# A hybrid decoder layer on one core: side work placed by a running plan of all engines in place of fixed delays, block states by scans, the samples' convolution taps by products, and no arithmetic left on GpSimd in the output projection

## The chip, the cores and the metric

The kernel runs on one core of one Trainium2 chip. The metric is device microseconds of one execution. The kernel before takes 1282.72 us, the median of 3 runs (1280.19 to 1284.27). A core has five instruction queues that run side by side and meet only at semaphores: PE (TensorE: matmuls and transposes), DVE (VectorE), ACT (ScalarE), POOL (GpSimd) and SP (SyncE, here DMAs alone). Each queue runs its own instructions in the order in which they were written. Arithmetic between engines goes through SBUF; PE writes PSUM banks, which ACT and DVE empty. DMAs are issued from SP and from POOL.

## The reference

One layer (`DEPTH = 1`) over 1024 prompt positions and 8 samples of 4 positions, width 1024. Both share all weights.

```python
mod = silu(c) @ w_ada + b_ada                       # shift, scale, gate, twice
h = rmsnorm(x, g_pre_mix) * (1 + sc1) + sh1
z = h @ w_in                                        # 24 blocks of 128 columns
za, zq, zf, zi, zg, zc = split(z)
ya = u * (tril(w_s) @ layernorm(v) + b_s)           # chunked gMLP, u, v = gelu(za)
# HGRN2, 8 heads of 64x64: per chunk with decay products b
#   o = (q*exp(b)) @ S + tril((q*exp(b)) @ (k*exp(-b)).T) @ v
#   S = exp(b_last) * S + (k*exp(b_last - b)).T @ v
yb = rmsnorm(o) * silu(zg)
yc = silu(layernorm(conv31(a * sigmoid(gate)) + b_dw))    # 31 taps per channel
y = concat(ya, yb, yc) @ w_out
x = x + gt1 * rmsnorm(y, g_post_mix)
h = rmsnorm(x, g_pre_mlp) * (1 + sc2) + sh2
x = x + gt2 * rmsnorm(square(relu(h @ w_up)) @ w_down, g_post_mlp)
```

The new states of HGRN2, the last convolution rows and the gMLP's v rows of the samples are returned too.

## The kernel before

All activations lie with features on the partitions: a tile of 128 x 1056 holds 128 features of the 1024 prompt and 32 sample positions, cut into three chunks `c` of 352 columns. Every large product is computed as three matmuls on a high and a low half of each operand (hi*hi, hi*lo, lo*hi), so a block of 128 output features and one chunk is 8 x 3 = 24 matmuls `pmt` of 352 columns. I count the program's place by these matmuls: 1728 of them make the input projection (24 blocks x 3 chunks), 576 the output projection (8 x 3, chunk by chunk, so chunk 0 ends at 1920, chunk 1 at 2112, chunk 2 at 2304), and 4608 the MLP. The first up-products of chunk 0 run from 2304 to 2400, those of chunk 1 from there.

Around this stream lies the side work, all of it written as Python generators in named queues (`queues`, `add_task`): the adaLN products (`ada`), for each of four pairs of HGRN2 heads the decay products (`stage`), transposes (`turned`: `vtps`, `ktps`), scores, states and outputs (`recur`: `sc`, `us`, `ob`, `uss`, `os_`) and the norm (`head_norm`: `gnps`), the convolution (`conv_taps`, `conv_tail`), the gMLP (`gmlp`), and after the output projection `after_mix` for each chunk: sum of squares `tot`, a matmul with ones (`stps`), square root on ACT, reciprocal and products on DVE, addition of x by an accumulating DMA from POOL (L1412), a copy to DRAM (L1415), squares `sq` of the sum, their fold, a second `stps`, then `h2{c}hi` and `h2{c}lo`, which the up-products read.

`product8` writes the 24 matmuls in four pieces of six and calls `step` after each. `step(t)` (L164) moves a clock forward by the time of a piece and resumes those generators whose due time has come and whose engines have credit. A generator says with `yield 11.0`, `yield settle(3.0, "act", "pool")` or `yield 6.5` after how many microseconds it wants to go on; `settle` adds what an engine is behind by its credit. `Metered` (L38) charges each instruction a price from its size (`dve_price`, `ActPrice`, `pool_price`, `pe_price`). So the place of a transpose or a small matmul in PE's queue comes from a fixed delay, not from when its operands are ready. If it stands too early, PE waits there, and with it the large products behind it.

PSUM banks for side work come from a pool of five (`pb`, tag `b`), those for `pmt` from a pool of three (`pm`). Small tiles (`rs`, tag `rs`) rotate over three buffers.

Two pieces of arithmetic that the change touches: the state of each 64-position block is computed on DVE in 16 steps of one instruction per pair (`S[:, b] = D64[b] * S[:, b-1] + u[b]`, read straight from PSUM, L1180 on), and copied by ACT in four parts for each head. And for the samples each of the 31 taps of the convolution is one DVE instruction on 8 x 4 columns beside the prompt's one of 1024 columns (L805 on). In the output projection the squares of a block's result are added up on POOL (`add_square(tot, ps, m, POOL)`), and a third of each of the chunks 0 and 1 is scaled there (`scaled(..., (2,))`).

## Time and profile before

| what | value |
|---|---|
| median of 3 runs | 1282.72 us |
| profiled execution, its own time | 1286.04 us |
| its span, first to last instruction | 1284.2 us |
| mean granted TensorE clock | 0.985 |
| PE busy | 1243.9 us (97%) |
| DVE busy | 729.9 us (57%) |
| ACT busy | 480.8 us (37%) |
| POOL busy | 91.0 us (7%) |

The profile is of one execution; the span leaves out 1.8 us of its own time. Nearly all instructions carry one line (L56), that of the helper `Metered`, so groups are told apart by the names of their tiles. A row of a group gives engine, operation, output<-inputs, shapes, count, busy time in all, mean nanoseconds of one, and the idle time ahead of them with what ended it. The busy time of PE counts a matmul until its modelled end, so neighbours overlap: what tells of PE is where it is idle, and how far apart matmuls start. PEclk is the clock that was granted to it, as a share of full speed.

### The profile page before, as it was taken

The page shows a single profiled execution, that of the slowest core. Times are in us where ns is not written, and L with a number is a line of the kernel's source. Part 1 is how long each engine was busy: PE and PEld are TensorE (multiplying, and loading weights), DVE is VectorE, ACT ScalarE, POOL GpSimd, SP SyncE. Part 2 cuts the span into 40 slices and gives each one's busy share as a digit, 9 for nine tenths or more (in the row PEclk, how much of TensorE's full clock was granted, in tenths as well). Part 3 has the DMA queues.
Part 4 walks back from the last instruction along what each step waited for, and adds up shares of the span by engine and source line. Part 5 has one row for each costly group of instructions (what it writes and reads, how often), then busy time and mean ns, then how long its engine had stood idle before and what let it go on. Part 6 is the DMA issues. An engine that isn't in the chain of part 4 may idle for free.

```text
span 1284.2 us, 20789 instructions
## 1 busy us (share of the span) xinstructions
PE 1243.9 (97%) x8770; PEld 1199.8 (93%) x8770; DVE 729.9 (57%) x1182; ACT 480.8 (37%) x890; POOL 91.0 (7%) x123
## 2 busy tenths in 40 slices
PE   9999999998999998799999999999999999999995
PEld 7888988997999998799999999999999999999994
DVE  5799898879768657745343333333333333433366
ACT  6512544665754745445320220320311311311333
POOL 0000020212010233000000000000000000000001
PEclk9999999999899999799999999999999999999998
DMA  9557240111111467143211111111111111110218
GB/s 363 177 146 291 74 184 24 36 58 46 34 43 52 150 176 207 48 128 107 82 50 50 36 48 50 50 50 36 47 50 50 36 48 50 50 50 34 90 18 207
DMA packets 39246, 113.24 MB, mean 88 GB/s; under 512 B 9952, under 2 KB 12160, under 8 KB 39024
## 3 DMA queue, kind: packets, MB, share of 16 engines
q1 hardware_dynamic: 34832, 99.22, 23.0%
q0 software_dynamic: 4320, 12.68, 4.4%
q8 instruction: 69, 1.13, 0.4%
q14 instruction: 25, 0.20, 0.0%
HBM read 101.75 MB, written 10.14 MB: 87 GB/s over the span
## 4 chain that ended last, share of the span: by engine, by line
PE 81%; DVE 8%; ACT 6%; issue 2%; DMA 2%; POOL 1%; SPq 0%; DVEq 0%; ACTq 0%; POOLq 0%
PE pmt L56 74%; PE adaps L56 1%; PE stps L56 1%; DVE acc L56 1%; DMA raw<-in_wup 1%; DMA o<-in_xT 1%; PE sc L56 1%; DVE wlo L56 1%; DVE o L56 1%; PE pmt L673 1%; DVE sq L56 1%; ACT sq L56 1%; ACT whi L56 1%; DVE R L56 1%; DVE q L56 1%
## 5 line engine op out<-in xcount | busy, mean ns | idle before, releaser
L56 PE MATMUL pmt<-ah,whi 128*128 128x352 f32 (+2 forms) x744 | 241.4, 324 | 0.0
L56 PE MATMUL pmt<-al,whi 128*128 128x352 f32 (+2 forms) x744 | 240.1, 323 | 0.3
L56 PE MATMUL pmt<-ah,wlo 128*128 128x352 f32 (+2 forms) x744 | 240.1, 323 | 0.0
L56 ACT CAST whi<-raw 128x1024 fp32r<-128x1024 f32 (+2 forms) x113 | 114.3, 1014 | 261.0 <-PE pmt L56 261.0
L56 DVE TENSOR_TENSOR acc<-acc,pmt 128x352 f32<-128x352 f32 (+2 forms) x176 | 87.8, 503 | 167.7 <-PE pmt L56 167.7
L56 DVE TENSOR_TENSOR wlo<-raw,whi 128x1024 fp32r<-128x1024 f32 (+2 forms) x113 | 136.5, 1210 | 70.0 <-ACT whi L56 69.9
L56 DVE TENSOR_TENSOR rsq<-relu 128x352 f32<-128x352 f32 x84 | 44.2, 526 | 188.4 <-ACT relu L56 188.4
L56 PEld LDWEIGHTS pmt<-al,whi 128*128 128x128 f32 x744 | 140.0, 188 | 1.6 <-DVE al L56 0.8
L56 PEld LDWEIGHTS pmt<-ah,whi 128*128 128x128 f32 x744 | 139.7, 188 | 1.1 <-ACT ah L56 0.3
L56 PEld LDWEIGHTS pmt<-ah,wlo 128*128 128x128 f32 x744 | 139.9, 188 | 0.4
L56 ACT ACTIVATE relu<-pmt 128x352 f32<-128x352 f32 x96 | 44.6, 464 | 237.1 <-PE pmt L56 237.1
L56 PE MATMUL pmt<-h22hi,wlo 128*128 128x352 f32 x256 | 82.6, 323 | 0.0
L56 PE MATMUL pmt<-h22hi,whi 128*128 128x352 f32 x256 | 82.5, 322 | 0.0
L56 PE MATMUL pmt<-h22lo,whi 128*128 128x352 f32 x256 | 82.3, 322 | 0.0
L56 PE MATMUL pmt<-h21lo,whi 128*128 128x352 f32 x232 | 75.3, 324 | 2.5 <-DVE h21lo L56 2.5
L56 DVE SCALAR_TENSOR_TENSOR cva<-cvx,vec_t,cva 128x1024 f32<-128x1024 f32 x60 | 76.7, 1279 | 0.1
L56 PE MATMUL pmt<-h21hi,whi 128*128 128x352 f32 x232 | 75.3, 325 | 1.0 <-ACT h21hi L56 1.0
L56 PE MATMUL pmt<-h21hi,wlo 128*128 128x352 f32 x232 | 75.1, 324 | 0.0
L56 PE MATMUL pmt<-h20hi,wlo 128*128 128x352 f32 x232 | 74.8, 322 | 0.0
L56 PE MATMUL pmt<-h20hi,whi 128*128 128x352 f32 x232 | 74.8, 322 | 0.0
L56 PE MATMUL pmt<-h20lo,whi 128*128 128x352 f32 x232 | 74.6, 322 | 0.0
L56 DVE TENSOR_TENSOR al<-rsq,ah 128x352 fp32r<-128x352 f32 x96 | 50.4, 525 | 26.9 <-ACT ah L56 17.8
(362 smaller groups left out, 2741.2 us busy)
## 6 DMA issues: line engine op xcount, KB each, us to landing
rawada<-in_wada SPq DMA_DIRECT2D x48, 512.0 KB, 7.9
raw<-in_wup SPq DMA_DIRECT2D x36, 512.0 KB, 3.5
raw<-in_wdn SPq DMA_DIRECT2D x36, 512.0 KB, 3.4
raw<-in_win SPq DMA_DIRECT2D x22, 512.0 KB, 3.6
raw<-in_wout SPq DMA_DIRECT2D x20, 512.0 KB, 3.6
x<-in_xT SPq DMA_DIRECT2D x6, 528.0 KB, 7.4
o<-in_xT POOLq DMA_DIRECT2D x6, 528.0 KB, 6.4
x1d<-o POOLq DMA_DIRECT2D x6, 528.0 KB, 7.6
```

What stands on the lines that cost most here:

```text
L56: return f(**kw)
L673: nc.tensor.matmul(out=pss[m, c], lhsT=r(w_first[m][i % 2][:, k, :]), rhs=r(h[c][i // 2][:, k, :]), start=k == i == 0, stop=k == 7 and i == 2)
```

## The change

- `Plan` keeps, while the program is written, a time at which each engine is free, each tile is written and each PSUM bank was last used. `Metered` reports every instruction to it with a price; SP's and POOL's DMAs are now metered too (POOL's: 0.9 us and 8 us until landed).
- `until(tiles, banks=n)` takes the place of the fixed delays and of `settle`: a generator waits until the plan has the tiles written and n of the last five banks free by PE's planned time.
- In `recur` the states are no longer computed step by step: ACT copies the two PSUM banks `us` to SBUF with the 16 blocks innermost, and spreads the decays (`decs`, the first set to 0); two scans of 128 x 512 on DVE run over (value column, block); ACT copies the states back, one copy for each head, and the last state to `hg_o`.
- In `conv_taps` every eighth step multiplies the 31-row history with the 31 weights for one of the 4 sample positions (128 x 248), and every second of these is followed by one reduction over the taps; the bias is added by ACT at the end.
- In the output projection the squares are added up on DVE, and all three parts are scaled on DVE. POOL keeps only DMAs there.

```diff
+class Plan:
+    def __init__(self):
+        self.free = dict.fromkeys(("pe", "act", "dve", "pool", "dma"), 0.0)
+        self.done, self.used, self.banks = {}, {}, []
+        self.moved = False
+    def now(self):
+        return self.free["pe"]
+    def given(self, key, price, out, ins, extra=0.15):
+        names = [x.tensor.name for x in ins]
+        end = max(self.free[key], self.now(), *(self.done.get(x, 0.0) for x in names)) + price
+        self.free[key] = end
+        out = out.tensor.name
+        self.done[out] = end + extra
+        for x in (out, *names):
+            self.used[x] = max(self.used.get(x, 0.0), end)
+        self.moved |= key == "pe"
+    def ready(self, aps, banks):
+        t = [self.done.get(x.tensor.name, 0.0) for x in aps]
+        if banks:
+            t.append(sorted(self.used.get(x, 0.0) for x in self.banks[-5:])[banks - 1])
+        return max(t) <= self.now() + 0.1
...
+            if op == "dma_start":
+                if self._key == "pool":
+                    self._plan.given("pool", 0.9, out, ins, 8.0)
+                else:
+                    self._plan.given("dma", out.shape[0] * n * 4 / 3e5, out, ins, 2.0)
+                return f(**kw)
...
-    def settle(extra, *keys):
-        return extra + max(0.0, *(-credit[k] for k in keys))
+    def until(*aps, banks=0):
+        while not plan.ready(aps, banks):
+            yield 0.2
...
         ACT.copy(out=sb[:, 0:512], in_=ps)
-        yield settle(1.5, "act", "pe")
+        yield from until(sb, banks=1)
         pt = pb.tile([128, 4, 128], F32, tag="b", name="adapt")
...
-                DVE.scalar_tensor_tensor(out=so, in0=sv, scalar=wc, in1=so, op0=ALU.mult, op1=ALU.add)
+            if tap % 8 == 0:
+                t = tap // 8
+                if t % 2 == 0:
+                    taps = rs("taps")[:, 0:496].rearrange("p (t b i) -> p t b i", t=2, b=8)
+                DVE.tensor_tensor(out=taps[:, t % 2], in0=hist[:, :, t:t + 31],
+                                  in1=rep(vc(V_WDW + 31 * j, 31), 8), op=ALU.mult)
+                if t % 2:
+                    DVE.tensor_reduce(out=so[:, :, t - 1:t + 1].rearrange("p b t -> p t b"), in_=taps, axis=AX.X,
+                                      op=ALU.add)
...
-        S = by_block(q2)
-        for b in range(16):
-            u = us[b // 8][:, b % 8, :]
-            if b == 0:
-                DVE.tensor_copy(out=S[:, 0, :], in_=u)
-            else:
-                DVE.scalar_tensor_tensor(out=S[:, b, :] if b < 15 else hg_o[:, p, :], in0=S[:, b - 1, :],
-                                         scalar=D64[:, b:b + 1], in1=u, op0=ALU.mult, op1=ALU.add)
-            if b % 4 == 3:
-                for hh in range(2):
-                    o, n = 64 * hh, min(b + 1, 15)
-                    ACT.copy(out=sv[hh][o:o + 64, b - 2:n + 1], in_=S[o:o + 64, b - 3:n])
-                yield
+        S = q2[:, 0:NP].rearrange("p (d b) -> p d b", b=16)
+        for i in range(2):
+            ACT.copy(out=S[:, :, 8 * i:8 * i + 8], in_=us[i].rearrange("p b d -> p d b"))
+        POOL.memset(D64[:, 0:1], 0.0)
+        yield
+        decs = rs("decs")
+        ACT.copy(out=decs.rearrange("p (d b) -> p d b", b=16),
+                 in_=D64.rearrange("p (o b) -> p o b", o=1).to_broadcast([128, 32, 16]))
+        for i in range(2):
+            u = q2[:, 512 * i:512 * i + 512]
+            DVE.tensor_tensor_scan(out=u, data0=decs, data1=u, initial=0.0, op0=ALU.mult, op1=ALU.add)
+        yield
+        for hh in range(2):
+            o = 64 * hh
+            ACT.copy(out=sv[hh][o:o + 64, 1:16], in_=S[o:o + 64, :, 0:15].rearrange("p d b -> p b d"))
+        ACT.copy(out=hg_o[:, p, :], in_=S[:, :, 15])
+        yield from until(vt, KE, k2, QE, banks=2)
         ob = [pb.tile([128, 8, 64], F32, tag="b", name=f"ob{i}") for i in range(2)]
-        yield settle(2.0, "dve", "act")
...
     def head_norm(p, st, oo, rd, hi, lo):
+        yield from until(hi, lo, banks=3)
...
-        yield 2.5
+        yield 1.0
+        yield from until(tot, banks=1)
         rstd = rstd_of(tot)
         yield
-        for kk in (normed(c, src, rstd, Go1) if c == 2 else scaled(c, src, rstd, (2,))):
+        for kk in (normed(c, src, rstd, Go1) if c == 2 else scaled(c, src, rstd, ())):
...
-        yield 14.0
+        yield from until(*(src(kk) for kk in range(3)))
         for d in sum_squares(src, box):
...
-            add_square(tot, ps, m, POOL)
+            add_square(tot, ps, m, DVE)
```

Further `until` calls stand ahead of the transposes in `turned` and `gmlp`, of `sc`, `us` and `uss` in `recur`, of the means in `conv_tail`, and after the loads in `ada` (`yield 7.0` and `until` for `yield 11.0`).

What this moves, at the three places that the prediction speaks of. First POOL's queue around chunk 1 of the output projection. `tot` and `sqb` are the sum of squares and a block's squares, `o_4732` to `o_4734` (now `o_4632` to `o_4634`) the three parts of the chunk's result. Before:

```order
L1415 DMA x1d<-o_4410 128x704
L56 TENSOR_TENSOR tot<-tot,sqb 128x352 x6
L1412 DMA o_4732<-in_xT 128x1056
L1412 DMA o_4733<-in_xT 128x1056
L56 TENSOR_TENSOR o_4734<-o_4734,rstd 128x704
L1412 DMA o_4734<-in_xT 128x704
L1415 DMA x1d<-o_4732 128x1056
```

Now:

```order
L107 DMA x1d<-o_4310 128x704
L107 DMA o_4632<-in_xT 128x1056
L107 DMA o_4633<-in_xT 128x1056
L107 DMA o_4634<-in_xT 128x704
L107 DMA x1d<-o_4632 128x1056
```

The six additions and the product have left the queue in which they stood behind the copies to DRAM.

Second, DVE at the change from the output projection to the MLP: the folds `sq` are of chunk 1, `tot` is of chunk 2, `h20lo` and `h21lo` are the MLP's inputs of chunks 0 and 1. Before:

```order
L56 TENSOR_TENSOR sq<-sq 128x1056
L56 TENSOR_TENSOR sq<-sq 128x704
L56 TENSOR_TENSOR sq<-sq 128x352 x2
L56 SCALAR_TENSOR_TENSOR h20lo<-o_4410,mod,h20hi 128x352 x2
L56 TENSOR_TENSOR tot<-tot,sqb 128x352
L56 RECIPROCAL rstd<-rstd 128x352
L56 TENSOR_TENSOR al<-rsq,ah 128x352
L56 RECIPROCAL rstd<-rstd 128x352
```

Now:

```order
L113 TENSOR_TENSOR sq<-sq 128x1056
L113 TENSOR_TENSOR sq<-sq 128x704
L113 TENSOR_TENSOR sq<-sq 128x352 x2
L113 TENSOR_TENSOR wlo<-raw,whi 128x1024
L113 TENSOR_TENSOR tot<-tot,sqb 128x352 x3
L113 RECIPROCAL rstd<-rstd 128x352
L113 TENSOR_TENSOR al<-rsq,ah 128x352
```

`h20lo` now ends ahead of the folds, and between chunk 1's folds and its own `h21lo` only one reciprocal stands; chunk 2's comes after them. On PE the `stps` of chunk 2's `tot` moves with it, from behind the 2322nd `pmt` to behind the 2400th; that of chunk 0's second sum moves from 2172 to 2088, chunk 0's first from 1944 to 1938, chunk 1's second from 2328 to 2322.

Third, PE between the third and the fourth pair of heads (`vtps` is the fourth pair's first transpose, `gnps` the third pair's norm). Before:

```order
L56 MATMUL vtps<-cst_t,vf 128x128 x8
L56 MATMUL pmt<-h0hi,whi 128x352
L56 MATMUL pmt<-h0lo,whi 128x352
L56 MATMUL pmt<-h0hi,wlo 128x352
...
L56 MATMUL shps<-cst_t,vf 32x128
L56 MATMUL gnps<-gnhi,means 128x352
L56 MATMUL gnps<-gnlo,means 128x352
```

Now the norm stands ahead of the transposes, and these are written in two halves:

```order
L113 MATMUL gnps<-gnhi,means 128x352
L113 MATMUL gnps<-gnlo,means 128x352
L113 MATMUL pmt<-h0hi,whi 128x352
L113 MATMUL pmt<-h0lo,whi 128x352
L113 MATMUL pmt<-h0hi,wlo 128x352
...
L113 MATMUL vtps<-cst_t,vf 128x128 x4
```

Six rows `gnps` follow each other there; 24 `pmt` lie between the last of them and the first `vtps`. The matmuls from `us` to `ob` of the four pairs are 36, 30, 30 and 30 `pmt` apart before, and 48, 48, 66 and 48 now.

## Prediction

> **What bounds the kernel now.** I read first the chain of waits and PE's idle time by stretch, then what PE waited for, then ACT, DVE and POOL at those places. In the chain, 96 matmuls `pmt` in a row take

> ```profile
> 384.93 15.37 PE pmt L56 x96
> ```

> so 0.160 us each; with that I turn places in PE's queue into time. The windows that follow (bounds; length, PE busy and instructions, granted clock, DMA share, GB/s) show the MLP and nine short stretches:

> ```profile
> 604.00:1256.00 652.00, 651.73 (x4041) 1.00 0.16 50
> 201.00:203.00 2.00, 0.19 (x2) 1.00 0.72 227
> 203.00:209.00 6.00, 5.12 (x26) 0.72 0.03 12
> 295.00:301.00 6.00, 3.31 (x56) 1.00 0.00 1
> 318.00:322.00 4.00, 0.78 (x4) 0.84 0.34 125
> 322.00:328.00 6.00, 6.00 (x24) 0.54 0.24 90
> 510.00:517.00 7.00, 0.33 (x3) 0.88 0.28 108
> 517.00:522.00 5.00, 4.62 (x12) 0.50 0.01 3
> 534.00:539.00 5.00, 2.54 (x15) 1.00 0.15 33
> 539.00:545.00 6.00, 5.03 (x17) 0.51 0.22 68
> ```

> From 604 us on PE has no gap and full clock; the change writes no instruction differently there, and so 650 us are out of reach. What can be won lies ahead of it. Idle time is length less busy time; a lower clock costs its missing share of the busy time. Around 201: 1.8 + 0.9 idle, and 6.0 x 0.28 = 1.7 by the clock, 4.4. Around 295: 2.7. Around 318: 3.2, and 6.0 x 0.46 = 2.8, together 6.0. These 13.1 us lie in the input projection. Around 510: 6.7 + 0.4, and 4.6 x 0.50 = 2.3, together 9.4. Around 534: 2.5 + 1.0, and 5.0 x 0.49 = 2.5, 6.0. PE's waits from 60 to 604 us (total, times, longest) name them:

> ```profile
> PE stps L56 <- DVE tot L56: 7.8, 2, 7.1
> PE gnps L56 <- ACT vf L56: 3.2, 1, 3.2
> PE adapt L56 <- ACT adasb L56: 2.7, 1, 2.7
> PE pmt L56 <- DVE h21lo L56: 2.5, 1, 2.5
> PE pmt L56 <- ACT sqb L56: 1.0, 2, 0.7
> PE pmt L56 <- ACT h21hi L56: 1.0, 1, 1.0
> ```

> The wait around 295 is for `ob` of pair three. The rest, 0.7 of `tot` and 1.0 of `sqb`, brings the handover from output projection to MLP to 17.1, and all to **30.2 us**. In each case a small matmul, or a first operand, is in PE's queue before its producer is done.

> At the handover I read POOL, ACT and DVE in time order (start, duration, what, idle time ahead and its end), from the `stps` of chunk 0's first sum:

> ```profile
> 445.36 0.75 PE L56 MATMUL stps<-tot,cst_t 128*128 128x352 f32 x2
> 455.01 2.04 POOL L56 TENSOR_TENSOR o<-o,rstd 128x704 f32<-128x704 f32 x1
> 457.35 0.87 POOL L1412 DMA_DIRECT2D o<-in_xT  x1 [0.30 <-POOL o L56]
> 467.79 0.54 POOL L1415 DMA_DIRECT2D x1d<-o  x1 [2.71 <-DMA o<-in_xT]
> 468.35 5.91 POOL L56 TENSOR_TENSOR tot<-tot,sqb 128x352 f32<-128x352 f32 x5
> 469.34 0.46 ACT L56 ACTIVATE sqb<-pmt 128x352 f32<-128x352 f32 x1 [7.28 <-POOL tot L56]
> 470.77 1.66 DVE L56 TENSOR_TENSOR wlo<-raw,whi 128x1024 fp32r<-128x1024 f32 x1 [10.02 <-ACT whi L56]
> 511.88 4.02 DVE L56 TENSOR_TENSOR sq<-sq 128x1056 f32<-128x1056 f32 x4
> 516.81 0.51 DVE L56 TENSOR_TENSOR tot<-tot,sqb 128x352 f32<-128x352 f32 x1
> ```

> POOL's additions `tot` stand behind copies that wait until an accumulating DMA has landed. ACT then has no buffer for the next square, waits 7.28 us, and holds up the weights, for which DVE waits 10.02. The same repeats for chunk 1; at the end DVE comes to chunk 2's `tot` at 516.81, behind the folds, and PE has waited 7.05 us for it.

> **The change part by part.** *Convolution taps and states.* DVE's rows, with the nearest for what is new:

> ```profile
> 60.00:410.00 350.00, 341.40 (x3063) 315.75 (x3062) 294.74 (x480) 173.71 (x341) 43.19 (x60) 0.99 0.28 93
> L56 DVE SCALAR_TENSOR_TENSOR cva<-cvhist,vec_t,cva 128x32 f32<-128x32 f32 x60 | 18.9, 315 | 0.0
> L56 DVE SCALAR_TENSOR_TENSOR q<-q,dec,us 128x64 f32<-128x64 f32 x56 | 15.7, 281 | 2.3
> L56 DVE TENSOR_TENSOR_SCAN f<-f,d 128x1056 f32<-128x1056 f32 x4 | 9.4, 2351 | 0.0
> L56 DVE TENSOR_TENSOR gmt<-gmps,rows 128x512 f32<-128x512 f32 x4 | 2.7, 687 | 0.2 <-PE gmps L56 0.2
> ```

> (The first row's pairs are PE, PEld, DVE, ACT, POOL.) About 36 us go, with a few of the 64-column kind. New are 8 scans of 512 columns: by the scan row 2.2 ns a column, 1.2 us each, 9.6; 8 products of 248 columns between 0.3 and 0.69 us, I take 0.4, 3.2; 4 reductions of 496, no row shows one, bounded by the 512-column product 0.69 from below and twice that from above, I take the lower, 2.8. DVE loses some 20 of 294.74 us. That alone is worth nothing, since DVE was idle a sixth of this stage; it helps by bringing `ob`'s operands sooner. ACT's copies change from sixteen small ones to five larger per pair; at half busy (173.71 of 350) it hides them, except in the chain from `us` to `ob`: two copies, the decays, two scans, two copies back, by ACT's and DVE's rates about 1.3 + 0.6 + 2.4 + 2.1 = 6.4 us, some of it behind one convolution tap or a 1.0 us copy. PE now has 48 `pmt` between, 7.7 us, in one pair 66. So each `ob` waits 0 to 1.5 us; I take 0.7, **3 us** for all four, nothing near what slows the clock. The other waits of the input projection go: the norm `gnps` stands 24 `pmt` (3.8 us) ahead of the transposes whose copies held its bank, `adapt` is no longer behind the copies of `vtps` in ACT's queue, `ob` of pair three has 10.6 us instead of 4.8. More splits in the stream (a half `vtps` here, a half `ktps` there) cost start-up, 0.2 us each by the six-matmul pieces beside them, **1 us**. So 13.1 become 4.

> *Chunk 0's second sum, moved 84 `pmt` (13.4 us) forward.* This is the place where the new order may be too early. DVE and copy rows, from groups by shape:

> ```profile
> L56 DVE TENSOR_TENSOR o<-o,rstd 128x1056 f32<-128x1056 f32 x4 | 4.8, 1248 | 0.0
> L56 DVE TENSOR_TENSOR x<-x,rstd 128x704 f32<-128x704 f32 x3 | 2.7, 887 | 0.0
> L56 DVE RECIPROCAL rstd<-rstd 128x352 f32<-128x352 f32 x10 | 23.5, 2352 | 20.0 <-ACT rstd L56 20.0
> L56 DVE TENSOR_TENSOR wlo<-raw,whi 128x1024 fp32r<-128x1024 f32 x107 | 133.8, 1250 | 70.0 <-ACT whi L56 69.9
> L56 ACT CAST whi<-raw 128x1024 fp32r<-128x1024 f32 x107 | 111.7, 1044 | 261.0 <-PE pmt L56 261.0
> L56 ACT ACTIVATE sq<-o 128x704 f32<-128x704 f32 x3 | 2.4, 791 | 0.0
> DMA to landing us min/median/max: 5.7/6.7/10.2
> ```

> (The last row is of the accumulating DMAs.) Before, the third was issued 457.35 - 445.36 = 12.0 us after `stps` and its copy began 10.4 later. Now the root, a reciprocal (2.35), two products of 1.25 with a weight split of 1.2 between and one of 0.89 make 8.4 with the handovers: 3.6 sooner, as POOL's product of 2.04 is gone. With the same 10.4 it lands 18.8 after `stps`. Then the square 0.8, two more of its sort on ACT, the next square and a weight copy (1.0), with their handovers 2.1, a weight split 1.2, the folds 4.0: 26.9. PE is there after 150 `pmt`, 24.0. So PE waits **3 us**, and at such waits (2.7 around 201, 3.2 around 318) the clock fell after, for 1.7 to 2.8; I take **2.2**. ACT's `sqb` no longer waits for POOL, and chunk 2's `tot` at 2400 is ready many microseconds early, so the 9.4 and the 1.8 go. The 18 additions (0.51 each, 9.2 us) and two products are hidden: DVE waited 10.02 us in a single piece here. Chunk 1's second sum, by the same steps, is done some 2 us before PE's place for it.

> [...]

> *Chunk 1's `h21lo`.* The chain ends at

> ```profile
> 517.38 1.54 PE stps L56 x2
> 540.04 1.08 DVE L56 SCALAR_TENSOR_TENSOR h21lo<-o,mod,h21hi 128x352 fp32r<-128x352 f32 x2 [0.16 <-ACT h21hi L56]
> ```

> so 23.7 us after its `stps`. One reciprocal (2.35) and about 1.2 us of waiting for it leave the chain: 20. PE reaches the last operand 78 + 21 matmuls after that `stps`, 15.8 us. It waits **4.2**, much as before (3.4), then **2.5** by the clock. Nothing in the change shortens this.

> *Sum.* 30.2 - 3 - 1 - (3 + 2.2) - (4.2 + 2.5) = 14.3 us off the profiled 1284.2 (with 1.8 around it 1286.04, itself 3.3 over the median): 1282.7 - 14.3 = **1268 us**.

> **Rivals.** *The accumulation lands sooner.* With the median 6.7 in place of 10.4 the second sum is ready at 23.2 and PE does not wait: 5.2 less, 1263. For it: POOL now issues without a pause. Against it: the third of each batch was among the slow ones while the weights stood still, and they flow now. If `h21lo` gains too, 1256. [...]

> *The plan is wrong about DVE.* It prices the scan of 1056 columns at 1.2 us, and the row says 2.35; where DVE is busy without a break, side products still come early, elsewhere. If that keeps 10 of the 13.1, and not 4, it is 1274 to 1278.

> *The accumulation lands later, and it gets slower.* ACT no longer stands still, so weights are fetched through the same 16 engines while chunk 0 and then chunk 1 are accumulated. A landing at 17 us, 7 later, costs 7 at chunk 0's sum, 5 at chunk 1's (2 of slack) and with the clock some 3 at each: 1286. It decides from 16 us on; no row is above 10.4.

> That the change does not do what it says is out: the order of the queues shows it.

> **How the numbers follow.** Chances: forecast 0.58 (1262 to 1274), sooner 0.15, plan wrong 0.16, later 0.11. Under about 0.3% (3.9 us) a difference is none that a measurement can tell. Faster: 0.58 + 0.15 + 0.08; same 0.08; slower 0.11. The range runs from 1255, where nothing but the splits and one microsecond is left of 30.2, to 1280.

> **What would show it.** Right: no wait of PE over 1.5 us and no clock under 1.0 between 60 and 400 us; `sqb` waits for no one; a wait of PE for `sq` of about 3 us at chunk 0's second `stps`, one of about 4 us for `h21lo`. Wrong: waits for `ob`, `gnps` or `vtps` over 2 us (the second rival); accumulating DMAs over 12 us, or under 8 at the third (the other two).

## The result and the profile after

The changed kernel takes 1270.31 us (median of 4, 1269.2 to 1271.25) against 1281.45 us of the kernel before beside it: ratio 0.9914, 95% interval 0.9886 to 0.9941. Forecast were 1268 us and a ratio near 0.989; 11 us came of the 14.3. The profiled execution has a span of 1268.7 us, 15.5 less than that of before; these two make the gain look larger than it is, since the profiled execution of before took 1286.04 us, 4.6 over its median here, and that of the changed kernel lies on its median. The 15.5 us are nearly all PE's idle time and lost clock between 55 and 604 us: 20.2 + 10.1 = 30.3 us before, 11.3 + 3.4 = 14.7 now. (I count idle stretches from 0.3 us, and for the clock the busy time of each microsecond times the share that wasn't granted.)

What PE waits for now, from 60 to 604 us (total, times, longest):

```profile
PE pmt L113 <- DVE gq L113: 3.5, 2, 2.6
PE ob L113 <- ACT K L113: 2.8, 4, 1.1
PE pmt L113 <- DVE h21lo L113: 2.4, 1, 2.4
PE stps L113 <- DVE sq L113: 2.1, 1, 2.1
PE pmt L113 <- ACT acc L113: 0.5, 1, 0.5
```

The waits for `tot`, `sqb`, `adapt`, `gnps` and `vf` are gone, as forecast. `ob`, `sq` and `h21lo` wait, as forecast. `gq` was on nobody's list. Three windows around the longest stalls and after them (length, PE busy and instructions, further engines, granted clock):

```profile
326.00:329.80 3.80, 1.18 (x9) 0.89 (x7) 2.78 (x4) 3.69 (x7) 0.00 (x0) 1.00 0.00 0
329.80:333.00 3.20, 3.20 (x13) 3.13 (x14) 3.20 (x6) 3.09 (x9) 0.00 (x0) 0.60 0.00 0
462.00:467.00 5.00, 2.88 (x18) 2.59 (x17) 4.65 (x6) 1.93 (x5) 0.00 (x0) 1.00 0.72 261
467.00:470.00 3.00, 3.00 (x10) 2.52 (x10) 1.96 (x3) 0.55 (x1) 0.00 (x0) 0.50 0.00 0
523.00:527.00 4.00, 1.61 (x9) 1.14 (x8) 2.08 (x6) 2.76 (x6) 0.00 (x0) 1.00 0.36 133
527.00:533.00 6.00, 6.00 (x39) 5.98 (x38) 5.93 (x11) 2.70 (x6) 0.89 (x1) 1.00 0.01 3
```

After the first and the second stall the clock fell to half, after the third (2.4 us, the second longest) it did not. Against the terms of the forecast:

| place | before | forecast | this profile |
|---|---|---|---|
| input projection, waits and clock | 13.1 | 4 | 8.0 (`ob` 2.8, `gq` 3.5 + 1.7) |
| chunk 0's second sum, wait + clock | (elsewhere) | 3 + 2.2 | 2.1 + 1.7 |
| chunk 1's `h21lo`, wait + clock | 3.4 + 2.5 | 4.2 + 2.5 | 2.4 + 0 |
| rest of the handover | 11.1 | 0 | 0.5 |
| together | 30.2 | 15.9 | 14.7 |

The sum was met by luck, because two errors cancel: the projection kept 4 us more, the handover 5 us less than forecast.

The chain of chunk 0's second sum, from the first `stps` to the second, in time order from PE, POOL, ACT and DVE:

```profile
439.83 0.75 PE L113 MATMUL stps<-tot,cst_t 128*128 128x352 f32 x2
447.74 1.75 POOL L107 DMA_DIRECT2D o<-in_xT  x2 [1.36 <-ACT whi L113]
459.68 0.79 ACT L113 ACTIVATE sq<-o 128x704 f32<-128x704 f32 x1 [1.94 <-DMA o<-in_xT]
461.16 1.05 ACT L113 CAST whi<-raw 128x1024 fp32r<-128x1024 f32 x1
462.24 1.23 DVE L113 TENSOR_TENSOR wlo<-raw,whi 128x1024 fp32r<-128x1024 f32 x1 [5.61 <-ACT whi L113]
463.38 3.30 DVE L113 TENSOR_TENSOR sq<-sq 128x1056 f32<-128x1056 f32 x4
466.74 1.32 PE L113 MATMUL stps<-sq,cst_t 128*128 128x352 f32 x2 [2.12 <-DVE sq L113]
```

From 439.83 to 466.74 are 26.9 us, the figure of the forecast. POOL issues the second and third accumulating DMA back to back from 447.74; the third is out about 8.8 us after `stps` and its data are there 11.1 us later (ACT's square at 459.68). Then stand square, weight copy, split and folds, one behind the other, as they were added up.

### The profile page after: what moved, and what is told of

Its sections match the earlier page's. It is cut to its first block, busy times and chain, and to the rows that moved or that the text cites. A ratio compares the mean times of both kernels' runs of the same rounds, so it can differ in the third digit from the quotient of the medians.

```text
span 1268.7 us, 20674 instructions
## 1 busy us (share of the span) xinstructions
PE 1237.8 (98%) x8770; PEld 1194.8 (94%) x8770; DVE 719.3 (57%) x1096; ACT 488.4 (38%) x882; POOL 63.0 (5%) x107
## 4 chain that ended last, share of the span: by engine, by line
PE 81%; DVE 9%; ACT 6%; issue 1%; DMA 1%; POOL 1%; ACTq 0%; DVEq 0%; POOLq 0%
PE pmt L113 74%; PE stps L113 2%; PE adaps L113 1%; DVE acc L113 1%; DVE vf L113 1%; DMA o<-in_xT 1%; DVE q L113 1%; ACT vf L113 1%; ACT K L113 1%; PE sc L113 1%; DVE wlo L113 1%; PE pmt L736 1%; ACT whi L113 1%; DVE y L113 1%; DVE R L113 0%
## 5 line engine op out<-in xcount | busy, mean ns | idle before, releaser
L113 DVE TENSOR_TENSOR al<-rsq,ah 128x352 fp32r<-128x352 f32 x96 | 50.4, 525 | 23.8 <-ACT ah L113 14.7
```

The lines of the kernel that those rows point to most:

```text
L113: return f(**kw)
```

## Experiments

All times stand beside the kernel before on the same chip (1280.15 us for the first four, 1277.24 for the next four, 1279.05 for the last three); ratios are to it. The changed kernel has 0.9914 (0.9886 to 0.9941) in its first runs and 0.9922 (0.9904 to 0.9941) beside the last three.

**Only the output projection's arithmetic.** The kernel before with

```diff
-        for kk in (normed(c, src, rstd, Go1) if c == 2 else scaled(c, src, rstd, (2,))):
+        for kk in (normed(c, src, rstd, Go1) if c == 2 else scaled(c, src, rstd, ())):
...
-            add_square(tot, ps, m, POOL)
+            add_square(tot, ps, m, DVE)
```

> The kernel before, with its fixed delays, states and taps; of the change only the output projection's arithmetic: squares added on DVE, all three parts scaled on DVE, POOL left with DMAs. Theory Q (POOL's queue is the cause at the handover: additions behind copies that wait for accumulating DMAs): the waits for tot of chunk 2 (7.1 us, 9.4 with the clock) and for sqb (1.8) go, the four waits of the input projection (13.1) and the one for h21lo (6.0) stay: 1281.5 - 11.2 = about 1270, so 9 to 12 us faster than before. Theory P (the plan's places on PE are the cause: the second sum earlier, chunk 2's sum later): the sum of chunk 2 still stands at the old place, and the time is within 4 us of before.

1275.79 us, 0.9966 (0.9954 to 0.9978): 4.4 us faster, not 9 to 12. From 60 to 604 us PE's longest waits at the handover are these two:

```profile
PE pmt L56 <- DVE h21lo L56: 2.6, 1, 2.6
PE pmt L56 <- ACT h20hi L56: 2.3, 1, 2.3
```

And this stands ahead of the second one on DVE and ACT:

```profile
501.09 3.30 DVE L56 TENSOR_TENSOR sq<-sq 128x1056 f32<-128x1056 f32 x4
504.92 1.08 ACT L56 ACTIVATE h20hi<-o,mod 128x352 fp32r<-128x352 f32 x2 [4.30 <-DVE o L56]
```

The waits for `tot` and `sqb` are gone, as theory Q says, but `h20hi` has taken the place: the last of chunk 0's operands stand on DVE behind chunk 1's folds and come 2.3 us after PE wants them. The run is also less clean than its diff: the delays of the old kernel look at DVE's credit, so two sums on PE moved with the edit, chunk 0's second from 2172 to 2196 (24 `pmt`, 3.8 us later) and chunk 1's first from 2136 to 2148. In its profile the handover loses 10.3 us instead of some 17 (5.7 of idle time, 4.6 by the clock); 4.0 of these, 2.3 and 1.7 by the clock, are at `h20hi`. POOL's queue was a cause, and behind it stood the place that delay and credit give chunk 0's sum; that an unmoved sum would have spared this wait is not shown. Neither theory holds alone, though the interval (2.8 to 5.9 us) takes in the 4 us that theory P allows.

**Only the output projection's arithmetic undone.** The changed kernel with the same two lines the other way round; on PE a single sum changes its place, chunk 1's second, which comes 6 `pmt` later (2328 for 2322).

> The changed kernel with the additions and the third product of a chunk back on POOL; PE's side products keep exactly the places that they have in the changed kernel. Theory Q: the additions queue behind the copies again, ACT's sqb waits over 5 us for POOL in chunks 1 and 2, DVE's weight splits and folds come late: the waits of PE at the handover, 5 us in the changed kernel, become 12 to 17: 1278 to 1283. Theory P: with these places the sums are met anyway; only the third product (2.04 us instead of 0.9) makes chunk 0's second sum 1 to 2 us later: 1271 to 1274.

1277.45 us, 0.9983 (0.9971 to 0.9996), 7 to 9 us slower than the changed kernel. PE's longest wait, and ACT's wait for POOL, from 410 us on:

```profile
PE stps L113 <- DVE sq L113: 8.1, 2, 4.7
ACT sqb L113 <- POOL tot L113: 8.2, 2, 5.1
```

Both second sums now wait, 4.7 and 3.4 us, and the handover loses 13.6 us with its clock, 7 more than in the changed kernel. Theory Q holds, with less than it had: it wanted 12 to 17 us of waits and 1278 to 1283, and there are 9.5 us of waits and a time just below. Theory P's 1271 to 1274 is out. So the plan's places are met only if POOL's queue is free: the arithmetic alone brings 4.4 us, everything else without it 2.7, both together 9 to 11.

**States and taps as before.** The changed kernel with the old loops for both (16 steps a pair; 31 instructions a block).

```diff
-        S = q2[:, 0:NP].rearrange("p (d b) -> p d b", b=16)
...
+        S = by_block(q2)
+        for b in range(16):
...
-                DVE.tensor_tensor(out=taps[:, t % 2], in0=hist[:, :, t:t + 31],
...
+                DVE.scalar_tensor_tensor(out=so, in0=sv, scalar=wc, in1=so, op0=ALU.mult, op1=ALU.add)
```

> The changed kernel with the old block states (16 steps a pair on DVE) and the old taps of the samples (31 instructions a block) in place of scans and products; plan and output projection as changed. Theory L (as I predicted: DVE's 20 us less are worth nothing by themselves, the plan places the side products by the load that there is): within 4 us of the changed kernel, 1267 to 1274, and since the convolution's tail comes later again, the wait for gq (3.5 us) is gone or elsewhere. Theory D (the DVE load was what made the side products early): the projection's waits come back in good part, 5 to 9 us: 1275 to 1280.

1273.73 us, 0.9958 (0.9943 to 0.9973): 3 to 6 us slower than the changed kernel. The waits at the handover are as there; the three longest in the projection:

```profile
PE gnps L113 <- ACT vf L113: 2.7, 1, 2.7
PE ktps L113 <- ACT y L113: 1.6, 1, 1.6
PE gmsp L113 <- DVE gvts L113: 1.5, 1, 1.5
```

The time is just inside what theory L allows, but the list speaks against my sentence that DVE's 20 us are worth nothing by themselves: `gq` and `ob` wait no more, and eight other waits, 9.6 us with 4.4 of clock, have come, 14.0 instead of 8.0. That is no less than in the kernel before (12.7 by the same count): in this profile the plan alone moved the waits of the projection and did not shrink them. Less DVE work is worth 3 to 6 us here, though DVE is idle a sixth of this stage. How much of it is load and how much only other places in the queues, this run doesn't tell apart.

**Where `gq` waits.** `gq` is a product of `pmt` with its sigmoid, and frees `pmt`'s bank. ACT in the changed kernel:

```profile
321.89 1.50 ACT L113 COPY vf<-vtps 64x256 f32<-64x256 f32 x4
323.30 1.27 ACT L113 ACTIVATE cva<-cva,vec_t 128x1056 f32<-128x1056 f32 x1
324.60 1.08 ACT L113 ACTIVATE y<-cva 128x1056 f32<-128x1056 f32 x1
325.59 1.26 ACT L113 ACTIVATE cva<-cva,vec_t 128x1056 f32<-128x1056 f32 x1
326.88 1.08 ACT L113 ACTIVATE y<-cva 128x1056 f32<-128x1056 f32 x1
327.99 0.82 ACT L113 ACTIVATE sgg<-pmt 128x352 f32<-128x352 f32 x2
```

Four long instructions of the convolution's tail stand ahead of two sigmoids whose banks PE needs at 327.1. Before, the tail came at 341 to 350 us, and with the old loops in the changed kernel at 336 to 342; less DVE work brought it forward into ACT's fullest stretch, and the queue of the convolution asks only for DVE's credit before it goes on. Two kernels change the delay of that part alone, once to 16 us and once to 8. The plan answers to it, so on PE side matmuls behind it move too, with 8 us the fourth pair's transposes by 12 to 42 `pmt`:

```diff
-        yield 2.0
+        yield 16.0
         for j in range(2):
             z = cva[j]
```

> The changed kernel; only the last part of the convolution's tail (four ACT instructions over 1056 columns, 4.7 us) waits 16 us instead of 2 before it is written. Theory T (PE's wait of 3.5 us for gq at 322 to 330 us comes from ACT, which is busy without a break from 315 to 335 because that tail stands between two halves of the fourth pair's transposes): the wait for gq goes, with its clock 5.2 us: 1264 to 1266. Theory C (ACT is full there with copies of transposes, square roots and table loads even without the tail): the wait stays at 2 us or more, or moves to the next pmt: 1268 to 1271.

1275.10 us, 0.9963 (0.9951 to 0.9974): slower than the changed kernel by 5 to 6 us. The wait for `gq` has fallen to 1.3 us, and a larger one has come:

```profile
PE pmt L113 <- ACT gvf L113: 7.7, 1, 7.7
348.84 1.26 ACT L113 ACTIVATE cva<-cva,vec_t 128x1056 f32<-128x1056 f32 x1
350.12 1.28 ACT L113 ACT_TABLE_LOAD   x1
354.80 1.28 ACT L113 ACT_TABLE_LOAD   x1
356.09 0.47 ACT L113 ACTIVATE gvf<-pmt 128x352 f32<-128x352 f32 x1
```

Its place was now after the first gelu, so that ACT loads the sigmoid's table and the gelu's again around it, 1.28 us each, and `gvf` has to wait for all of that. The same cause at another bank.

> The changed kernel; the last part of the convolution's tail waits 8 us, not 2 and not 16: its four ACT instructions then stand behind both halves of the fourth pair's transposes and the last sigmoid, and ahead of the first gelu, so that ACT loads no further table. Theory T (the wait for gq is ACT's tail in the wrong place): no wait of PE over 1.5 us between 300 and 360 us; 3 to 5 us less than the changed kernel, 1264 to 1267 where before is 1281. Theory C (ACT is overfull there; whichever place is taken, some pmt or ob waits): a wait of 2 us or more turns up behind the tail, and the time is within 2 us of the changed kernel or above it.

With 8 us: 1266.40 us, 0.9907 (0.9887 to 0.9928). The longest wait in the projection is one of 1.5 us, `gq` has 1.3, and no clock is lost there:

```profile
PE ob L113 <- ACT K L113: 3.2, 4, 1.5
PE pmt L113 <- DVE gq L113: 1.3, 1, 1.3
522.00:528.00 6.00, 6.00 (x23) 6.00 (x23) 5.93 (x11) 1.34 (x3) 0.89 (x1) 0.53 0.01 3
```

So the wait of 2.6 us came from ACT's tail, as theory T says. But the time lies where theory C had it, within 2 us of the changed kernel (0.9907 beside 0.9914 and 0.9922): the gain is not to be told from nothing. In this profile the clock fell after `h21lo` (the last row) and cost 3.1 us, where in the changed kernel's it had not.

**The two sums at the handover.** `early` lets a generator go on so much before the plan's time (after it where negative): chunk 0's second sum 18 `pmt` later, chunk 1's 18 earlier.

```diff
-        yield 1.0
+        yield 14.0 if c == 2 else 1.0
         yield from until(tot, banks=1)
...
-        for d in sum_squares(src, box):
+        for d in sum_squares(src, box, (-2.4, 6.0, 0.0)[c]):
```

> The changed kernel with two small matmuls of the handover moved by 18 large ones (2.9 us) each: chunk 0's second sum later, chunk 1's second sum earlier; chunk 2's sum stays where it is (by a later start), so DVE has chunk 1's normalization ahead of three other products. The predicted mechanism (that sum is 2 to 3 us too early, and the chain behind chunk 1's sum ends 2.4 us after PE wants its last operand) says: the wait of 2.1 for sq and the clock's 1.7 go, the wait of 2.4 for h21lo goes: 6 us less than the changed kernel, 1263 to 1266. Rival: chunk 0's operands come too late for the first up-product, or chunk 1's folds aren't done at the earlier place: a wait of the same size elsewhere, 1268 to 1271.

1268.98 us, 0.9924 (0.9899 to 0.9950): no gain. In the input projection all is as in the changed kernel; at the handover both predicted waits are gone and one has come that is nearly as large as both. DVE there, and for comparison the same work in the changed kernel:

```profile
PE stps L113 <- DVE sq L113: 4.1, 1, 4.1
500.13 1.23 DVE L113 TENSOR_TENSOR wlo<-raw,whi 128x1024 fp32r<-128x1024 f32 x1 [2.61 <-ACT whi L113]
501.71 3.29 DVE L113 TENSOR_TENSOR sq<-sq 128x1056 f32<-128x1056 f32 x4
```

```profile
499.48 1.26 DVE L113 TENSOR_TENSOR sq<-sq 128x1056 f32<-128x1056 f32 x1 [1.82 <-ACT sq L113]
500.99 2.02 DVE L113 TENSOR_TENSOR sq<-sq 128x704 f32<-128x704 f32 x3 [0.25 <-ACT sq L113]
502.93 1.22 DVE L113 TENSOR_TENSOR wlo<-raw,whi 128x1024 fp32r<-128x1024 f32 x1
```

In the first of these two profiles, the new order, chunk 1's folds are written behind a weight split. The split waits for ACT's copy of the weights, the folds, whose squares are done, wait with it, and PE asks for them 18 `pmt` (2.9 us) earlier. The rival is right.

> The edits of the two kernels with the tail at 8 us and with the two sums moved, together. If both mechanisms hold they lie in different stages and add: 9 to 11 us less than the changed kernel, 1258 to 1262; what is left of PE's idle time after 60 us is the four ob (2.8 us) and half a microsecond in the first down-products. If one of them only moves its wait, 1263 to 1267.

Both edits together: 1264.84 us, 0.9896 (0.9875 to 0.9917). It has the waits of both kernels, `ob` 3.2, `gq` 1.3 and the 4.2 of chunk 1's sum: one of the two only moved its wait, and the time lies where that was expected.

**`ob` 1 us later.**

```diff
-        yield from until(vt, KE, k2, QE, banks=2)
+        yield from until(vt, KE, k2, QE, banks=2, early=-1.0)
         ob = [pb.tile([128, 8, 64], F32, tag="b", name=f"ob{i}") for i in range(2)]
```

> The changed kernel; only the four ob wait until the plan's time is 1 us past their operands (the plan prices a scan of 512 columns at 0.64 us and a spread copy of 960 at 0.9). Of the changed kernel's 2.8 us of waits for ob under 1 stay; the rest of the projection is shifted by it, though, and the tail of the convolution stands before other instructions. Theory S (a local price): 2 us less, 1266 to 1269. Theory R (a shift of a few matmuls anywhere in the projection makes new waits elsewhere of the same order): 1268 to 1274 with other waits in the list.

1264.47 us, 0.9892 (0.9871 to 0.9912), the best so far and better than either theory had it. Of the waits for `ob` 2.0 are left, and `gq` is no longer among the waits at all, since in the shifted order the convolution's tail stands elsewhere; no wait of the projection is over 1.1 us. The gain is mostly theory R's shift, here to the good. Once more, beside the changed kernel unaltered and a kernel with a smaller shift of the sums:

> The changed kernel, unaltered, as the measure for the kernels beside it on this chip (before took 1280 on one chip and 1277 on another). Expected: 0.991 of before, and the same stalls as in its first profile to 0.1 us; if each stall of 2 to 3 us costs the clock in some executions and not in others, the clock's loss differs from the 3.4 us of that profile while the stalls do not.

> The kernel with the four ob 1 us later, once more beside the changed kernel: if its gain is its own, it is 2 to 5 us below the changed kernel on the same chip; if the chip made it, it is within 1 us.

1270.45 us for the changed kernel (0.9922) and 1265.40 us (0.9893, 0.9873 to 0.9913) for the later `ob`: 5 us, its own and not the chip's. And the changed kernel's second profile has the same three longest stalls as its first (2.6, 2.2 and 2.4 us) and no lost clock at all; at `ob` and `sc` it waits 1.4 us more, so not all of the 3.4 us of clock is won. Both over the same two stretches, the first profile's rows ahead:

```profile
329.00:333.00 4.00, 3.26 (x13) 3.19 (x14) 4.00 (x8) 3.87 (x11) 0.00 (x0) 0.68 0.00 0
466.00:470.00 4.00, 3.26 (x10) 2.79 (x11) 2.93 (x5) 0.55 (x1) 0.00 (x0) 0.63 0.07 30
```

```profile
PE pmt L113 <- DVE gq L113: 3.5, 2, 2.6
PE stps L113 <- DVE sq L113: 2.2, 1, 2.2
329.00:333.00 4.00, 3.68 (x23) 3.33 (x23) 4.00 (x7) 3.89 (x10) 0.00 (x0) 1.00 0.05 10
466.00:470.00 4.00, 3.88 (x22) 3.67 (x23) 3.39 (x5) 0.56 (x1) 0.00 (x0) 1.00 0.00 0
```

**The best of it.** The later `ob` with

```diff
+        yield 14.0 if c == 2 else 1.0
...
+        for d in sum_squares(src, box, (-1.2, 3.0, 0.0)[c]):
```

> The kernel with the four ob 1 us later, and at the handover chunk 0's second sum 6 large matmuls later, chunk 1's 6 earlier, chunk 2's first sum kept where it was. The second sum's stall should fall from 2.1 to about 1.1 us, short of what costs the clock (no stall under 1.6 us did in any profile so far): 1.0 and 1.7 saved. For h21lo: one product fewer stands inside its chain and the chain starts 1 us earlier: 2.4 falls to 0 to 1. Together 4 us less than the kernel with the later ob alone. Rival: the earlier second sum of chunk 1 meets folds that are not done (as when it was moved by 18): no gain, or 1 to 3 us lost.

1263.22 us (1262.90 to 1264.39), 0.9871 (0.9852 to 0.9890): 7 us less than the changed kernel beside it, 2 less than the later `ob` alone.

```profile
PE pmt L113 <- ACT h21hi L113: 2.1, 1, 2.1
PE stps L113 <- DVE sq L113: 1.2, 1, 1.2
```

The second sum's wait fell as worked out, to 1.2 us without a loss of clock. That of chunk 1's operands fell by 0.3 only, and in this profile cost 1.6 us of clock: PE now waits for the high half instead of the low one. Half of the expected 4 us came.

## Why the prediction was right, and where it was not

- **What bounds the kernel, and the 30.2 us within reach: right.** 604 to 1240 us have 635.73 us of PE busy time before and 635.86 after, and what was won came from idle time and clock ahead of it. But the 30.2 us are of one execution, 3.3 us over the median, and I took the 14.3 off the median: the profiles differ by 15.5, the medians by 11.
- **POOL's queue as the cause at the handover: right, in part.** Giving the arithmetic back costs 7 to 9 us. Alone, without the sum's new place, it brings 4.4 and not the 11.2 that the waits for `tot` and `sqb` add up to; 4.0 of what is missing is the wait for `h20hi` with its clock. The forecast had both parts and never had to ask.
- **Chunk 0's second sum: right.** 26.9 us were forecast and measured. The landing took 11.1 us, not 10.4, and the issue 8.8, not 8.4; other steps gave 1 us back, so that the sum agrees to a tenth is luck. PE came at 24.8 and not at 24.0, so it waited 2.1 instead of 3. The first rival (landing in 6.7) and the last (17) fell with this row.
- **Chunk 1's `h21lo`: right mechanism, wrong size.** On PE:

```profile
507.12 0.76 PE L113 MATMUL stps<-sq,cst_t 128*128 128x352 f32 x2
520.17 0.75 PE L113 MATMUL stps<-tot,cst_t 128*128 128x352 f32 x2
526.53 0.43 PE L113 MATMUL pmt<-h21lo,whi 128*128 128x352 f32 x1 [2.39 <-DVE h21lo L113]
```

  The chain took 19.4 us against 20 forecast, but PE came to the last operand 17.0 us after `stps`, not 15.8: I counted only `pmt`, and two sums, of 0.75 us each (they overlap their neighbours), stand there too. So 2.4 and not 4.2.
- **The clock's 2.2 and 2.5: wrong as certainties.** Each was paid in some profiles and not in others (below).
- **The input projection at 4: wrong.** My own sign, no wait over 1.5 us and no lost clock before 400 us, failed at `gq` with 2.6 us. `ob` was right in sum (2.8 for 3). That the other waits go was right, but I concluded from ACT's half load that it hides what is moved onto it. Load over a stage says nothing of its fullest part: from 316 to 335 ACT was busy for 18.6 of 19 us, with a tail that had moved there because DVE was faster. The second rival (the plan early elsewhere) had the size, 10 against 8.0, and put it on DVE.
- **DVE's 20 us worth nothing by themselves: not borne out.** The run with the old loops is 3 to 6 us slower, though it doesn't tell load from places. The price of a scan was met, 1.2 us, that of the copies back was not: 1.9 us each, and I had 2.1 for both. They read 960 columns 16 apart; that this is why was not shown.

```profile
L113 DVE TENSOR_TENSOR_SCAN q<-decs,q 128x512 f32<-128x512 f32 x8 | 9.3, 1204 | 2.5 <-ACT decs L113 2.5
L113 ACT COPY vf<-q 64x960 f32<-64x960 f32 x4 | 7.7, 1913 | 11.8 <-DVE q L113 11.8
```

## What to carry to other kernels

An engine that is half idle over a stage can still be full for 19 us of it, and PE waits there: when work is removed from one engine, look at where the work behind it moves to, and what the other engines do in just that stretch. An order that is planned from when operands are ready is worth its full gain only if no queue holds them up, and the other way round: the parts taken alone brought 4.4 and 2.7 us here, together 9 to 11. And in a stream whose small waits are all near each other, removing one by a shift can make others: judge a place only with its neighbours, and by a time taken beside the kernel that it is compared with.

## What I had not expected of the hardware

The same stall cost the clock in one profile and not in another. Over the 13 profiles of this case, by the length of PE's idle stretch (lost: a clock under 1.0 in the 12 us after; stalls under 1.1 us are left out):

| stall of PE | stalls | followed by a lower clock |
|---|---|---|
| 1.1 to 1.6 us, none longer within 12 us | 11 | 0 |
| 1.9 to 2.7 us | 27 | 14 |
| over 2.7 us | 8 | 8 |

Where it is lost, the loss is 1.5 to 1.7 us (3.4 us at half clock) or 2.4 to 3.1 (two or three times as long, some of it idle). The stall of 2.6 us for `gq` lost 1.7 in the changed kernel's first profile and nothing in its second, with the same program. A stall of 1.9 to 2.7 us was enough in 14 of 27 cases, so it wasn't its length alone that decided.

Most of what the executions of the kernel before differ by on one chip goes with the clock. Of 26 there, the fastest took 1276.79 us at a mean clock of 0.988, the slowest 1283.10 at 0.983; 0.005 of 1280 us are 6.4 us, and the two differ by 6.3 (correlation over the 26: -0.91). So a profile with a lucky clock shows a gain that isn't there: by the profiled spans the kernel with only the output projection's arithmetic is 13 us below the one before (1271.0 and 1284.2, on two chips), by the medians 4.4. With 14 of 27 stalls of 1.9 to 2.7 us followed by a lower clock, half of the clock's price is what I would have had to expect for each.
